# Splitting two output weights beside the first pass, and loading the parts at the change to the output pass

## The chip, the cores and the metric

The kernel runs on one core of a Trainium2 chip. The metric is the device time of one execution in microseconds (us). Engines are named as in the profile: PE (matrix products), DVE (vector), ACT (scalar), POOL (GpSimd) and SP, which here only starts transfers (DMAs). Each engine runs its instructions in the order of its own queue.

## The reference, cut to what matters

```python
def encoder_layer(x, ...):                      # 4096 + 2048 tokens, 1024 channels, float32
    h = rms_norm(x, pre_g)
    proj = jnp.einsum('bsd,de->bse', h, w_in)   # first pass: projections
    a_u, a_v, a_gate, b_in, b_gate, c_in, c_gate = jnp.split(proj, offsets, axis=-1)
    ya = mixer_a(a_u, a_v, ...) * jax.nn.silu(a_gate)
    yb = mixer_b(b_in, ...) * jax.nn.silu(b_gate)
    yc = mixer_c(c_in, c_w) * jax.nn.silu(c_gate)
    y = jnp.einsum('bse,ed->bsd', jnp.concatenate([ya, yb, yc], axis=-1), w_out)   # output pass
    return x + rms_norm(y, post_g)
```

## The kernel before

Big products are computed by a scheme with seven products in place of eight, called P1, P2, X1, X2, Y1, X3 and Y2. Each of the seven multiplies a sum of quadrants of the tokens by a sum of quadrants of the weights. To keep float32 accuracy, every factor is split into a high and a low part: `split` (L135 to L138) casts the source to the high part on ACT (L137) and subtracts it from the source on DVE (L138). `mm3` (L140) then makes three matmuls: high by high (L141), high by low (L142), low by high (L143).

The program has stages. The **first pass** takes 12 blocks of 512 tokens and ends near 485 us. The **b and a passes** follow until about 1358 us, in an order written by hand. The **output pass** takes 24 groups of 256 tokens, called q 0 to q 23, and ends the program. In the first and the output pass a scheduler of the compiler lays out each engine's queue from the order of the program and its own model of time.

In the first pass each block needs the statistics of its tokens. `row_squares(b+1)` is called in block b after P1. It loads four rows tiles (`xrow`, L362), each of which ACT squares in two halves with a sum (L365). The tiles take turns in a ring of **two** buffers (tag `xrow`). `statistics(b+1)` is called after X1: a sum and a scaling on DVE (L349, L351), a power on POOL (`rr`, L353), four diagonals on DVE (`diag`, L377), two matmuls that spread them (`prb`, L378), and a copy by ACT (`rbc`, L382). `normaliser` then multiplies the next block's operands (`xp`, L398) on DVE. The matmul outputs, `prb` among them, take turns in eight PSUM banks, given out in the order of the program.

Beside the blocks, `run_background` advances generators that prepare weights, one step after P2 and one after X3 of each block. `sum_weights("o", i, ...)` loads two rows tiles of the output weight (`wso0a` to `wso3b`, L741 and L742), makes four sums on POOL (L157 to L160), and stores the four results to `wall_o` in DRAM (L749).

At the change to the output pass, `load_out_weights` (L1513) loads each product's four summed tiles into places left by earlier weights (L1516), and `cut_out_weights` (L1519) splits each on the chip (L1522). The places have names such as `woY1h`, `woY2l`, `wol1`, `wo_more`. They name a place and not the product that uses it. The output group's operands (`yo_P`, `yo_Y`, `yo_X`) are made from `y` tiles loaded at L1533 and L1534, and split by ACT with DVE or POOL. Group q 0 also loads `pgb` (L1685) and scales it on DVE (L1686).

Of the kernel before, what the change touches and what calls it, by code (L numbers as in the profile page):

```python
# [10 lines left out]
F32 = mybir.dt.float32  # L11
F32R = mybir.dt.float32r
# [3 lines left out]
P = 128  # L16
D = 1024
NK = D // P
TB = 512
# [14 lines left out]
def hybrid_encoder(  # L34
# [33 lines left out]
    nc = tc.nc  # L68
# [6 lines left out]
    def pool(name, bufs):  # L75
        return phase.enter_context(tc.tile_pool(name=name, bufs=bufs, reuse_waits="tile"))
# [7 lines left out]
    w0g, wpa, e0, rpool, e1 = pool("w0g", 2), pool("wpa", 12), pool("e0", 1), pool("rpool", 1), pool("e0b", 1)  # L84
    hpool, xpool = pool("hpool", 6), pool("xpool", 8)
    dpool = ctx.enter_context(tc.tile_pool(name="dpool", bufs=1, space=DRAM))
# [22 lines left out]
    vn_d = dpool.tile([NTOK // P, P, 384], F32, name="vn_d")  # L109
    wb_d = dpool.tile([3, P, 1024], F32, name="wb_d")  # L110
    wall_d = {n: dpool.tile([7, P, c, TB], F32, name=f"wall_{n}") for n, c in (("b", 3), ("a", 3), ("o", 4))}
    z_d = [dpool.tile([s, 256], F32, name=f"z_d{i}") for i, s in enumerate(SEQS)]
    gc_d = [dpool.tile([256, s], F32, name=f"gc_d{i}") for i, s in enumerate(SEQS)]
    ya_d = [dpool.tile([384, s], F32, name=f"ya_d{i}") for i, s in enumerate(SEQS)]
# [21 lines left out]
    def split(src, hi, lo, pool_lo=False):  # L136
        last_cast[0] = nc.scalar.copy(hi, src)  # L137
        return (nc.gpsimd if pool_lo else nc.vector).tensor_sub(lo, src, hi.bitcast(F32))  # L138
# [16 lines left out]
    def weight_sums(b11, b12, b21, b22, eng):  # L155

        eng.tensor_sub(b11, b12, b11)  # L157
        eng.tensor_sub(b12, b22, b12)
        eng.tensor_sub(b22, b22, b11)
        eng.tensor_sub(b21, b21, b22)  # L160
# [247 lines left out]
    def row_tile(name):  # L408
        return rpool.tile([P, D], F32, tag="wrow", name=name, bufs=2)
# [325 lines left out]
    def place(name, m, i):  # L735
        return wall_d[name][OUT_ORDER.index(m)][:, i]

    def sum_weights(name, i, ra, rb):

        a, b_ = row_tile(f"ws{name}{i}a"), row_tile(f"ws{name}{i}b")  # L740
        nc.sync.dma_start(a, ra)  # L741
        nc.sync.dma_start(b_, rb)  # L742
        if name == "o":
            quads = a[:, W_H0], a[:, W_H1], b_[:, W_H0], b_[:, W_H1]
        else:
            quads = a[:, W_H0], b_[:, W_H0], a[:, W_H1], b_[:, W_H1]
        weight_sums(*quads, nc.gpsimd)
        for m, q in zip(("Y1", "X2", "X3", "X1"), quads):
            nc.sync.dma_start(place(name, m, i), q)  # L749
        yield  # L750

    background.extend(fold_pool_weights(h) for h in range(4))
    background.extend(sum_weights("b", t, wb_d[t], w1[2 + t]) for t in range(3))
    background.extend(sum_weights("a", t, w2[t], w2[3 + t]) for t in range(3))
    background.extend(sum_weights("o", k, w_o[k], w_o[k + 4]) for k in range(4))

    for b in range(NB):
# [755 lines left out]
    def load_out_weights(m):  # L1513
        hi, lo = ([next(place_of) for _ in range(4)] for _ in range(2))
        for k in range(4):
            nc.sync.dma_start(lo[k].bitcast(F32), wall_d["o"][OUT_ORDER.index(m)][:, k])  # L1516
        wo_raw[m] = hi, lo

    def cut_out_weights(m):  # L1519
        hi, lo = wo_raw.pop(m)  # L1520
        for k in range(4):
            split(lo[k].bitcast(F32), hi[k], lo[k])  # L1522
        wo[m] = list(zip(hi, lo))

    def load_y(q, yp=None):
# [52 lines left out]
    for b in range(NB // 2):  # L1578
# [42 lines left out]
        if b < NB // 2 - 1:  # L1621
            nxt = MixBlock(b + 1)
            ld[5].append(lambda n=nxt: n.load_v(0))
        else:
            for i, m in ((2, "P1"), (3, "X1"), (4, "P2"), (6, "X2")):
                ld[i].append(lambda m=m: load_out_weights(m))
                if m != "X2":
                    ct[i + 1].append(lambda m=m: cut_out_weights(m))
            ld[3].append(lambda: first_y.extend(load_y(0)))
            fb[5].append(next_y)  # L1630
            fb[6].append(next_y)
# [9 lines left out]
    prev.gate(0)  # L1641
    flush(stores)
    cut_out_weights("X2")
    assert at[0] > len(steps) + 1
    by_hand.close()
# [5 lines left out]
    for m in ("Y1", "X3", "Y2"):  # L1651
        load_out_weights(m)
        cut_out_weights(m)
        if m == "Y1":
            next_y()
# [241 lines left out]
```

## Time and profile before

| what | value |
|---|---|
| median of 3 runs | 1843.7 us |
| lowest and highest of them | 1839.59 and 1850.41 us |
| the profiled execution, its own time | 1844.26 us |
| its span, first to last instruction | 1842.5 us |
| mean granted TensorE clock (1 is 2.4 GHz) | 0.975 |
| PE busy | 1737.2 us, 94% |
| DVE busy | 1386.5 us, 75% |
| ACT busy | 915.9 us, 50% |
| POOL busy | 427.5 us, 23% |

An idle time in brackets stands at the instruction that ended it, with the engine and line that it had waited for. A busy share over the whole span mixes stages with different limits, so stretches are read one by one. PE is the fullest engine.

### The profile page before, as it was taken

How to read it: one execution, taken by the hardware profiler on the slowest of the kernel's cores; microseconds unless marked ns; L12 is line 12 of the kernel's file. 1: busy time of each engine (PE TensorE's matmuls, PEld its weight loads, DVE VectorE, ACT ScalarE, POOL GpSimd, SP SyncE). 2: the span in 40 equal slices, each digit the busy share in tenths (PEclk: the TensorE clock that was granted, in tenths of full speed). 3: DMA queues.
4: the chain of work that ended last, by engine and by line, in shares of the span. 5: the costliest groups of instructions: out<-in, count | busy, mean ns of one | idle time of the engine just before them, and what ended most of it. 6: DMA issues, size and time to landing. Idle time of an engine off the chain costs nothing. (4 is left out here: it accounts for less than half of the span.)

```text
span 1842.5 us, 27621 instructions
## 1 busy us (share of the span) xinstructions
PE 1737.2 (94%) x9784; PEld 1498.0 (81%) x9784; DVE 1386.5 (75%) x2320; ACT 915.9 (50%) x1766; POOL 427.5 (23%) x293
## 2 busy tenths in 40 slices
PE   5999999999998989799889999999989999999998
PEld 4999999999877777688677888778867888888886
DVE  8877777898588887667766677667776777777786
ACT  4766664335454554445545665646663433434332
POOL 5001121231000000000010100100115566665664
PEclk9999999999999999999899999999989999999999
DMA  6999997786868886879687577665934454454543
GB/s 248 324 335 342 350 358 273 278 309 250 281 227 272 279 306 246 275 273 306 231 291 266 198 241 255 221 219 168 310 124 161 161 170 162 160 170 162 171 149 114
DMA packets 221146, 443.83 MB, mean 241 GB/s; under 512 B 29776, under 2 KB 112336, under 8 KB 221008
## 3 DMA queue, kind: packets, MB, share of 16 engines
q1 hardware_dynamic: 221008, 442.07, 69.8%
q8 instruction: 77, 1.26, 0.3%
q14 instruction: 61, 0.50, 0.1%
HBM read 297.81 MB, written 150.47 MB: 243 GB/s over the span
## 5 line engine op out<-in xcount | busy, mean ns | idle before, releaser
L1421 POOL TENSOR_TENSOR lnst<-lnst,mhalf 128x16 f32<-128x16 f32 x12 | 38.2, 3180 | 525.5 <-DVE lnst L1420 289.2
L1729 POOL TENSOR_TENSOR cc<-cc,xr 128x1024 f32<-128x1024 f32 x46 | 110.3, 2398 | 53.5 <-DVE cc L1728 53.5
L398 DVE SCALAR_TENSOR_TENSOR xp<-xp,g_sb,rbc 128x256 f32<-128x256 f32 x192 | 97.5, 574 | 4.7 <-ACT rbc L382 3.2
L1432 ACT ACTIVATE vn<-vn,lnst 128x96 f32<-128x96 f32 x192 | 71.0, 456 | 43.7 <-DVE lnst L1427 42.5
L1670 ACT ACTIVATE junk<-cc 128x512 f32<-128x512 f32 x72 | 45.5, 632 | 86.0 <-DVE cc L1711 49.9
L137 ACT CAST yo_X<-y 128x512 fp32r<-128x512 f32 x60 | 34.9, 620 | 91.5 <-PE Xo L143 75.5
L138 DVE TENSOR_TENSOR yo_P<-y,yo_P 128x512 fp32r<-128x512 f32 x48 | 70.0, 1458 | 7.6 <-ACT yo_P L137 7.4
L1274 POOL MEMSET zb<- 128x16 f32 x6 | 0.5, 111 | 315.6 <-ACT zb L1272 254.3
L353 POOL TENSOR_TENSOR rr<-ssq,mhalf 128x4 f32<-128x4 f32 (+1 forms) x13 | 17.8, 1370 | 205.4 <-DVE ssq L351 118.5
L1728 DVE SCALAR_TENSOR_TENSOR cc<-cc,orr,pgb 128x512 f32<-128x512 f32 x69 | 53.8, 807 | 15.2 <-POOL orr L1678 15.2
L365 ACT ACTIVATE xrow<-xrow 128x512 f32<-128x512 f32 x88 | 54.9, 627 | 20.9 <-DMA xrow<-in_x_sample 20.0
L138 DVE TENSOR_TENSOR yo_X<-y,yo_X 128x512 fp32r<-128x512 f32 x48 | 58.9, 1226 | 0.2
L137 ACT CAST yo_P<-y 128x512 fp32r<-128x512 f32 x48 | 29.4, 615 | 47.1 <-PE Xo L143 26.1
L177 DVE TENSOR_TENSOR ys<-y,y 128x512 f32<-128x512 f32 x24 | 24.6, 1028 | 33.1 <-DMA y<-yc_d 32.9
L1417 DVE BATCH_NORM_STATS2 lnst<-vn 128x6 f32<-128x96 f32 x192 | 44.2, 230 | 6.3 <-ACT vn L1432 6.0
L1670 ACT ACTIVATE junk<-Po 128x512 f32<-128x512 f32 x24 | 14.4, 599 | 68.1 <-PE Po L143 68.1
L141 PE MATMUL pd<-mt,o 128*128 128x256 f32 (+1 forms) x80 | 27.0, 338 | 21.6 <-DMA mt<-const_m 18.6
L141 PE MATMUL Ab<-b_X1h,wbX1h 128*128 128x512 f32 x72 | 32.0, 444 | 15.7 <-ACT zb L1337 12.0
L1678 POOL TENSOR_TENSOR orr<-oms,mhalf 128x1 f32<-128x1 f32 x48 | 27.0, 563 | 84.1 <-DVE oms L1676 84.1
L1245 ACT COPY pa<-pb 32x512 f32<-32x512 f32 (+1 forms) x24 | 14.8, 619 | 56.6 <-DVE pb L1233 32.2
L1441 PE MATMUL pm<-ws,vn 128*32 128x128 f32 x1152 | 39.9, 290 | 2.8 <-ACT vn L1432 2.8
L1441 PEld LDWEIGHTS pm<-ws,vn 128*32 128x32 f32 x1152 | 34.6, 117 | 8.4 <-ACT vn L1432 5.5
(742 smaller groups left out, 6730.4 us busy)
## 6 DMA issues: line engine op xcount, KB each, us to landing
op_d<-xp SPq DMA_DIRECT2D x72, 512.0 KB, 5.1
mt<-const_m SPq DMA_DIRECT2D x56, 512.0 KB, 7.0
xp<-in_xt SPq DMA_DIRECT2D x48, 512.0 KB, 6.0
out<-cc SPq DMA_DIRECT2D x46, 512.0 KB, 2.9
xr<-in_x_sample SPq DMA_DIRECT2D x32, 512.0 KB, 4.3
xrow<-in_x_sample SPq DMA_DIRECT2D x28, 512.0 KB, 5.7
o<-o_d SPq DMA_DIRECT2D x40, 256.0 KB, 6.4
vn_d<-vg SPq DMA_DIRECT2D x48, 192.0 KB, 4.0
```

What stands on the lines that cost most here:

```text
L137: last_cast[0] = nc.scalar.copy(hi, src)
L138: return (nc.gpsimd if pool_lo else nc.vector).tensor_sub(lo, src, hi.bitcast(F32))
L141: nc.tensor.matmul(ps, lh, rh, start=first, stop=False, skip_group_check=True)
L365: nc.scalar.activation(half, half, AF.Square, accum_out=ss[:, 2 * c + h : 2 * c + h + 1])
L398: nc.vector.scalar_tensor_tensor(xs[q][:, sl], xs[q][:, sl], g8_sb[:, 4 * kh + k : 4 * kh + k + 1], rbc[a], ALU.mult, ALU.mult,)
L1417: nc.vector.bn_stats(st[:, j], self.v[h][c][:, 96 * hd : 96 * hd + 96])
L1421: nc.gpsimd.tensor_tensor(rv, va, mhalf, ALU.pow)
L1432: nc.scalar.activation(v_, v_, AF.Identity, bias=nb[:, j : j + 1], scale=rv[:, j : j + 1])
L1441: nc.tensor.matmul(pm[32 * hd : 32 * hd + 32, c * P : (c + 1) * P], self.v[h][c][:, 96 * hd + 32 * t : 96 * hd + 32 * t + 32], ws[:, hd], ...
L1670: nc.scalar.activation(junk, src, AF.Square, accum_out=ss[:, j : j + 1])
L1728: nc.vector.scalar_tensor_tensor(cc[c][:, hs], src, rr, pgb[:, hs], ALU.mult, ALU.mult)
L1729: nc.gpsimd.tensor_add(cc[c], cc[c], xr[c])
```

## The change

For the products Y1 and X3 of the output weight, `sum_weights` now also makes the high part beside the first pass. It takes a tile `whi` from the **same ring** as the `xrow` tiles, casts the sum into it on ACT, subtracts on DVE in place, and stores the high part to a new DRAM tensor `high_o`. `wall_o` then holds the low part for these two. `load_out_weights` loads the high part from there, and `cut_out_weights` leaves these two out. In all, 8 casts, 8 subtractions and 8 stores of 256 KB are added to the first pass, and at the change to the output pass 8 casts and 8 subtractions go and 8 loads of 256 KB come. Lines move by 2 (to about L748) and then by 6 to 9.

```diff
+    READY = ("Y1", "X3")
+    high_d = dpool.tile([len(READY), P, 4, TB], F32, name="high_o")
...
         for m, q in zip(("Y1", "X2", "X3", "X1"), quads):
+            if name == "o" and m in READY:
+                hi = e0.tile([P, D], F32, tag="xrow", name=f"whi{m}{i}", bufs=2)[:, 0:TB]
+                split(q, hi.bitcast(F32R), q.bitcast(F32R))
+                nc.sync.dma_start(high_d[READY.index(m)][:, i], hi)
             nc.sync.dma_start(place(name, m, i), q)
...
             nc.sync.dma_start(lo[k].bitcast(F32), wall_d["o"][OUT_ORDER.index(m)][:, k])
+            if m in READY:
+                nc.sync.dma_start(hi[k].bitcast(F32), high_d[READY.index(m)][:, k])
...
         for k in range(4):
-            split(lo[k].bitcast(F32), hi[k], lo[k])
+            if m not in READY:
+                split(lo[k].bitcast(F32), hi[k], lo[k])
```

The scheduler then lays out other queues. On PE before, in block 8 of the first pass, the two matmuls of the statistics of block 9 (`prb9`) stand between the gate columns (`Xg8`) of product X1 and the first matmul of X2.

```order
L143 MATMUL Xg8_4068<-p8_X1h_3958,wgX1l_181 128x256
L378 MATMUL prb9_4099<-diag9_0_4100,ident_146 128x256
L378 MATMUL prb9_4099<-diag9_1_4104,ident_146 128x256
L141 MATMUL Xc8_0_4042<-wtX2h_182,p8_X2h_4026 128x320
L142 MATMUL Xc8_0_4042<-wtX2l_183,p8_X2h_4026 128x320
```

On PE after, in the same block, they stand behind X3 (which now comes ahead of Y1), at the start of Y1 and within it.

```order
L145 MATMUL Xg8_4093<-p8_X3h_4176,wgX3l_194 128x256
L380 MATMUL prb9_4124<-diag9_0_4125,ident_147 128x256
L143 MATMUL Yc8_0_4180<-wtY1h_187,p8_Y1h_4114 128x320
...
L144 MATMUL Yc8_1_4193<-wtY1l_188,p8_Y1h_4114 128x320
L380 MATMUL prb9_4124<-diag9_1_4129,ident_147 128x256
L145 MATMUL Yc8_1_4193<-wtY1h_187,p8_Y1l_4115 128x320
```

So the statistics of block 9 stand some two products later, and X3 has moved ahead of Y1. The reason is seen on SP and ACT. On SP after, in the same block, the loads of the rows of block 9 (`xrow9`) are started between those of the weights (`wso2a`, `wso2b`), those of block 10's operands (`xp_10`) and the stores of the block's result (`z_d1`).

```order
L364 DMA xrow9_1_3984<-in_x_prompt 128x1024
L744 DMA wso2b_4048<-in_w_o 128x1024
L314 DMA xp_10_0_4373<-in_xt 128x1024
L314 DMA xp_10_1_4375<-in_xt 128x1024
L364 DMA xrow9_2_3988<-in_x_prompt 128x1024
...
L536 DMA z_d1_119<-ks1c8_1_3969 128x128
L364 DMA xrow9_3_3992<-in_x_prompt 128x1024
L755 DMA wall_o_116<-wso2a_4047 128x512
```

Before, all the `xrow` loads up to those of block 11 stood in the queue during blocks 3 to 5: the last, `xrow11_3`, stands just behind the stores of block 5. On ACT after, the squares of block 9 and the casts of the weights of steps 2 and 3 (`whiY12` is product Y1 of step 2) stand ahead of `rbc9` and of the first operand of block 9 (`p9_P1h`).

```order
L367 ACTIVATE xrow9_2_3988,ss8_9_3979<-xrow9_2_3988 128x512 x2
L139 CAST whiY12_4055<-wso2a_4047 128x512
L367 ACTIVATE xrow9_3_3992,ss8_9_3979<-xrow9_3_3992 128x512 x2
L139 CAST whiX32_4061<-wso2b_4048 128x512
L139 CAST whiY13_4307<-wso3a_4299 128x512
L535 ACTIVATE vg8_2_3926<-ku3c8_0_4170 128x192
L535 ACTIVATE vg8_3_3927<-ks1c8_1_3969 128x192
L384 COPY rbc9_4123<-prb9_4124 128x512
L139 CAST p9_P1h_4279<-xp_9_0_3915 128x1024
```

Nothing of the kind stood there before: ACT had `rbc9` right ahead of the cast `p8_Y2h`, with no squares and no weight casts near it.

On ACT before, at the change to the output pass (the operands `yo0` are those of q 0), the weight casts stand between the casts of the operands.

```order
L137 CAST yo0_Y1_13415<-ys3_0_13219 128x512
L137 CAST woY2l_13401<-wol1_13424 128x512 x2
L137 CAST yo0_Y1_13415<-y2_0_12942 128x512
L137 CAST woY1h_13291<-woY2h_13400 128x512
L137 CAST woY1l_13399<-woY2h_13400 128x512 x2
L137 CAST yo0_P2_13354<-y1_0_12941 128x512
...
L137 CAST woY1l_13399<-woY2l_13401 128x512
L137 CAST wol1_13424<-wol2_13425 128x512 x2
L137 CAST yo0_Y2_13487<-y2_0_12942 128x512
```

On ACT after, at the same place, eight of them are gone.

```order
L139 CAST yo0_Y1_13444<-ys3_0_13252 128x512
L139 CAST yo0_Y1_13444<-y2_0_12975 128x512
L139 CAST yo0_P2_13387<-y1_0_12974 128x512
...
L139 CAST woX3h_13322<-woX3l_13323 128x512 x2
L139 CAST woX3h_13322<-woY1h_13324 128x512
L139 CAST woX3l_13323<-woY1h_13324 128x512
L139 CAST yo0_Y2_13512<-y2_0_12975 128x512
```

The operands' casts move up by as many. DVE loses the eight subtractions that belong to them.

## Rows read from the trace of the kernel before

**Rows 1.** Page, busy time, share and instructions of PE and ACT.
```profile
PE 1737.2 (94%) x9784; PEld 1498.0 (81%) x9784; DVE 1386.5 (75%) x2320; ACT 915.9 (50%) x1766; POOL 427.5 (23%) x293
```

**Rows 2.** Windows: PE, PEld, DVE, ACT, POOL busy us; granted clock; DMA share; GB/s.
```profile
100.00:200.00 100.00, 100.00 (x735) 99.71 (x734) 73.61 (x138) 66.77 (x145) 7.29 (x4) 1.00 0.96 331
300.00:400.00 100.00, 95.03 (x674) 93.93 (x673) 83.36 (x119) 42.99 (x70) 26.36 (x19) 0.98 0.81 296
...
1370.00:1375.00 5.00, 3.82 (x9) 1.96 (x7) 5.00 (x10) 4.16 (x9) 1.77 (x1) 0.50 0.72 240
...
1400.00:1500.00 100.00, 99.89 (x437) 81.46 (x437) 77.48 (x95) 37.32 (x83) 63.99 (x43) 1.00 0.52 169
```

**Rows 3.** Waits of PE, 200 to 480 us: total, times, longest.
```profile
PE Pc L141 <- ACT ks1c L542: 6.5, 4, 2.3
PE Xc L141 <- ACT p_X1h L137: 2.7, 2, 1.5
```

**Rows 4.** Timeline of PE at a stop: start, us, instruction.
```profile
307.94 0.41 PE L141 MATMUL Pc<-wtP2h,p_P2h 128*128 128x320 f32 x1 [2.33 <-ACT ks1c L542]
...
309.20 0.47 PE L142 MATMUL Pc<-wtP2l,p_P2h 128*128 128x320 f32 x1
309.47 0.47 PE L143 MATMUL Pc<-wtP2h,p_P2l 128*128 128x320 f32 x1
```

**Rows 5.** Tile xrow, 100 to 480 us: duration in ns, minimum/median/maximum.
```profile
L365 ACT ACTIVATE xrow<-xrow x60: 612/625/647, 103.1 to 279.6; 128x512 f32<-128x512 f32 x60
L362 SPq DMA_DIRECT2D xrow<-in_x_prompt x16: 328/384/1412, 171.2 to 265.3; - x16
...
DMA to landing us min/median/max: 3.6/5.9/8.4
```

**Rows 6.** Groups of DVE, 100 to 480 us: busy us, mean ns.
```profile
L377 DVE TENSOR_SCALAR diag<-ident,rr 128x128 f32<-128x128 f32 x32 | 11.0, 393 | 2.2 <-PE prb L378 1.9
L559 DVE TENSOR_TENSOR ks1c<-Xc,ks1c 128x320 f32<-128x320 f32 x22 | 10.7, 485 | 1.4 <-PE Xc L143 1.3
...
L351 DVE TENSOR_SCALAR ssq<-ssq 128x4 f32<-128x4 f32 x8 | 1.3, 168 | 0.1
```

**Rows 7.** Line L353, 100 to 480 us, as rows 5.
```profile
L353 POOL TENSOR_TENSOR rr<-ssq,mhalf x8: 1006/1007/4274, 117.3 to 313.7; 128x4 f32<-128x4 f32 x8
```

**Rows 8.** Timeline of POOL, the last weight step.
```profile
422.32 1.78 POOL L157 TENSOR_TENSOR wso3a<-wso3a 128x512 f32<-128x512 f32 x1 [7.72 <-DMA wso3a<-in_w_o]
```

**Rows 9.** Timelines of DVE and ACT, normalising block 8's operands.
```profile
332.44 6.75 DVE L398 SCALAR_TENSOR_TENSOR xp<-xp,g_sb,rbc 128x256 f32<-128x256 f32 x9
...
338.91 1.05 ACT L137 CAST p_P2h<-xp 128x1024 fp32r<-128x1024 f32 x1 [7.70 <-DVE xp L398]
```

**Rows 10.** Timeline of PE at the change to the output pass.
```profile
1363.73 0.39 PE L143 MATMUL Xo<-woX1l,yo_P 128*128 128x512 f32 x1
1364.62 0.50 PE L141 MATMUL Yo<-woY1h,yo_Y 128*128 128x512 f32 x1 [0.50 <-ACT woY1h L137]
1368.39 0.80 PE L142 MATMUL Yo<-woY2h,yo_Y 128*128 128x512 f32 x1 [3.28 <-DVE woY2h L138]
...
1373.72 0.79 PE L141 MATMUL Po<-woP1h,yo_Y 128*128 128x512 f32 x1 [1.12 <-ACT yo_Y L137]
...
1387.81 0.80 PE L141 MATMUL Xo<-woY2l,yo_Y 128*128 128x512 f32 x1 [1.79 <-DVE u3o L1709]
...
1392.11 0.40 PE L143 MATMUL Xo<-woX1h,yo_X 128*128 128x512 f32 x1
```

**Rows 11.** Timeline of ACT at the same place.
```profile
1362.39 1.14 ACT L137 CAST woY2l<-wol 128x512 fp32r<-128x512 f32 x2
```

**Rows 12.** Timelines of POOL, SP and DVE at the same place.
```profile
1373.23 5.91 POOL L138 TENSOR_TENSOR yo_Y<-y,yo_Y 128x512 fp32r<-128x512 f32 x1 [41.02 <-DMA y<-ya_d]
...
1380.16 0.37 SPq L1685 DMA_DIRECT2D pgb<-in_post_g  x1
...
1386.46 0.69 DVE L1686 TENSOR_SCALAR pgb<-pgb 128x1024 f32<-128x1024 f32 x1 [7.89 <-issue]
```

## The prediction

> **What bounds the kernel now.** I read the busy shares first [rows 1]: PE is busy for 94% of the span, the next engine, DVE, for 75%. So the time moves where PE stops or runs slowly, and only there. The windows [rows 2] show where that is. From 100 to 200 us PE never stops, and its 735 matmuls give 0.136 us each, so one product of 36 matmuls takes 4.9 us. From 300 to 400 us it stops for 5 us. The output pass runs full. Between 1370 and 1375 us the granted clock is 0.50, the lower of the two levels (1.2 GHz). The waits of PE [rows 3] say what the first pass loses: 6.5 + 2.7 = 9.2 us in six waits from 200 to 480 us, all on ACT. The longest of them [rows 4] shows the second price of a stop: after 2.33 us without work, the matmuls of 320 columns start 0.27 us apart, and 12 or so of these, each 0.13 us above the mean of 0.136, make 1.6 us. At the change to the output pass [rows 10] the matmuls from 1363.73 to 1392.11 take 28.4 us; full speed is 100 / 437 = 0.229 us apart [rows 2], and the 62 of them would take 14.2. So the change costs about 14 us now. Its largest stop, 3.28 us, is for a weight's low part on DVE.
>
> **The change part by part: the casts and subtractions added.** Eight casts cost ACT about 0.57 us each (two took 1.14, [rows 11]), eight subtractions about as much on DVE. That is 4.6 us an engine, and ACT is idle for half of the span. I cost these at nothing by themselves. What counts is the ring they stand in.
>
> **The statistics of block 9.** The tiles `whi` of steps 0 and 1 stand in the two-buffer ring ahead of the rows tiles of block 9. Before, the squares of all blocks were over by 279.6 us [rows 5], some 60 us ahead of block 8's end. Now the four rows tiles of block 9 are loaded and squared within block 8, and the last load stands on SP behind two stores that need the end of Xc_1 X3 (the second half of the columns of product X3). From that end, PE still has the 12 gate matmuls of X3, 12 × 0.136 or about 1.5 us (they are the shorter ones), and then `prb9`. The path to `prb9` is: the last sum `ks1c`, 0.5 [rows 6]; two issues on SP at about 0.4 each (an issue took 0.37, [rows 12]), 0.8; the load, 5.9 in the median [rows 5]; two squares of 0.63, 1.3; two small operations of DVE at 0.17 [rows 6], 0.3; the power on POOL, 1.0 [rows 7]; two diagonals at 0.28 to 0.39, 0.7 [rows 6]. The sum is 10.5, less 1.5 for the cover: a stop of 9.0 us. With the shortest load of [rows 5], 3.6, it is 6.7; with the longest, 8.4, it is 11.5. The X3 matmuls were pulled ahead of Y1, so nothing is left behind them to fill it: Y1 needs a bank given out after `prb9`. Behind a stop of this length I count 2 us of slow matmuls (1.6 after the shorter stop of [rows 4]); bounds 0 and 3.
>
> The Trainium skill (DMA: Bandwidth & Descriptors, Anatomy of one DMA) fits 2.0 us plus the bytes over 436 GB/s to a DMA of GpSimd's path. For 512 KB that is an estimate of 3.2 us, and by it the stop would be 6.3 us and my forecast 1853 us. The median here, of SP's transfers with other transfers in flight, is 5.9, so the measurement decides and that sentence moves no term.
>
> **The operands of block 9.** The copy `rbc9` stands on ACT behind the cast of weight step 3, which waits for a load that starts only after step 2's stores. The last time, POOL waited 7.7 us for that load [rows 8]. With `prb9` at 10.5 after the end of Xc_1 X3, I put `rbc9` at about 17. PE has Y1 and Y2 until about 10.5 + 2 + 9.8 = 22.3. The first operand needs four multiplications and a cast and a subtraction, about 5 us: there in time. The second, P2, needs up to nine multiplications more, which took 6.75 us [rows 9], plus its cast and subtraction (2.2): ready at about 31.3, where P1 ends at 27.2. That is 4 us, and bounds of 0 and 6. In the trace of before ACT also waited for P2's operand, 7.70 us [rows 9], but there the chain began early enough. The X1 operand's cast then comes late too: 2 us, the size of the waits there now (2.7 in two, [rows 3]); bounds 0 and 3.
>
> **Other blocks.** Block 8 itself gets a cast and a subtraction ahead of its `ks1c` and `xp` work: +1 (0 to 2). Block 10's wait of P2, 1.6, goes (the four waits of [rows 3] are 1.0 to 2.3) and a wait of X1 of 1.0 comes: −0.6. Blocks 5 to 7 lose the squares and loads that stood there, and P2 is no longer cut in two by X1: the wait of 2.33 us at 307.94 [rows 4] goes, for −2 (0 to −4). The first pass sums to 9.0 + 2 + 4 + 2 + 1 − 0.6 − 2 = +15.4.
>
> **The change to the output pass.** ACT loses eight casts, 4.6 us, DVE eight subtractions, some 5 us. The stops of 0.50 and 3.28 us [rows 10] were for these. What is late next: the operand `yo_Y`, whose low part DVE makes after the casts (1.5), the low part of a remaining weight (0.5), the first matmul of P1 of q 1, whose `y` tile is loaded behind all weights, two more than before on that way (about 2; the cast of an operand from `y` held PE for 1.12 at 1373.72, [rows 10]), and half clock again for part of it. The last stop, 1.79 us on `u3o`, hangs on a chain of its own [rows 12]: POOL's `yo_Y` until 1379.1, then a `y` load, `pgb` at 1380.16, and its scaling at 1386.46. That chain starts from a cast on ACT which now comes some 2 to 3 us earlier, and it is bounded by that. Of the 14 us lost I take 4 back, with bounds of 2 and 6 (the whole of 0.50 + 3.28 and about 2 of slow clock).
>
> **Sum.** 15.4 − 4 = +11.4 on the profiled execution's 1844.26 us, which is 0.56 above the median of the runs. So 1855 us as a median. With every first-pass term at its low bound, the stop of 6.7 and nothing else but the −4.6 of the other blocks, and 6 back at the change, it is −3.9, or 1840; at the high bounds, 11.5 + 3 + 6 + 3 + 2 − 2 = +23.5, or 1867.
>
> On the slow matmuls, the rows show: PE without work for 2.33 us, then starts 0.27 us apart, about twice the mean of 0.136 [rows 2, 4]. The Trainium skill (TensorE: Matmul & The Clock Gate, The HAM clock gate) says that the clock of TensorE falls to 1.2 GHz when it idles. By this a stop costs more than its length, which speaks against the change, and each of the stops counted above (9 and 4 us) would pay it once; I have counted it for the first alone, and by both the sum would be 1857.
>
> **Rivals.** *The chain is hidden.* If the row loads land early, because the stores ahead of the last one go out at once, and the operands of block 9 are in time, only 6.7 stays, with 1 of slow clock, 1 in block 8, less 2.6: +6. Less 4 that is 1846, no change. For it: 3.6 us is a landing that was seen [rows 5], and PE's order gives P1 a good lead. Against: the DMA share is 0.81 there [rows 2]. *The chain comes back.* Blocks 10 and 11 have their rows just in time as well. If the stop comes again at block 10, at half its size, with late operands, +7: 1862. Against: their `prb` stand one product later than the last load. *Faster.* The six waits on ACT, 9.2 us, and their slow matmuls, some 4, come from a first pass in which squares and loads of later blocks share ACT and the queues with the blocks' own work (DMA share 0.96, [rows 2]). Moving them out could free all of it, and 6 come back at the change: 6.7 − 13 − 6, or −12, 1832; with half of it −6, 1838. It decides if the stop is below 6 us. Against: of the six waits only one lies in blocks that lose squares. *Nothing is saved at the change*, because the `y` and `pgb` loads take over at once: 1859. It is part of the range.
>
> **Chances.** The forecast 0.44, its own range 1849 to 1862; hidden 0.25; comes back 0.19; faster 0.12. A change within 0.5%, 9.2 us, can't be told from none. Of the forecast's 0.44 a quarter lies below 1853, so slower is 0.33 + 0.19 = 0.52; faster is three quarters of the last, 0.09; the rest, 0.39, is no change. The range takes in the forecast, the hidden chain and most of the one that comes back: 1842 to 1865.
>
> **What would show it.** Right: PE idle for 7 to 11 us before `prb9` in block 8 (waiting for DVE's `diag`), with a DMA `xrow` and ACT squares at the end of the chain; PE waiting for the P2 operand of block 9; the first pass longer by about 15 us; the 62 matmuls of the change in 22 to 26 us. Wrong: `prb9` without a wait of over 4 us, a first pass no longer than before, or a change to the output pass below 20 us.

## The result: 0.67% slower, at 1854.2 us

| | median | lowest to highest | ratio to before, 95% interval |
|---|---|---|---|
| before | 1841.49 us (8 runs) | 1838.18 to 1850.41 | |
| with the change | 1854.18 us (8 runs) | 1849.25 to 1862.38 | 1.0067 [1.0046, 1.0087] |

The profiled executions span 1842.5 and 1853.2 us. Cut into six stages on PE's timeline, the 10.7 us between them come from these:

| stage | before | after | difference |
|---|---|---|---|
| start to the first product (P1) of block 8 | 339.86 | 334.29 | −5.57 |
| block 8 | 36.67 | 56.44 | +19.77 |
| blocks 9 to 11 | 109.00 | 111.75 | +2.75 |
| b and a passes, to the first `Xo` | 875.70 | 872.14 | −3.56 |
| change to the output pass (first `Xo` to the last row of [rows 10]) | 30.88 | 27.63 | −3.25 |
| rest | 450.39 | 450.95 | +0.56 |

The first place to look is who PE waits for. This is the view of waits for PE from 200 to 480 us with the change, in total, times and longest, beside [rows 3].

```profile
PE prb L380 <- DVE diag L379: 8.5, 1, 8.5
PE Pc L143 <- ACT ks1c L544: 7.2, 4, 4.5
PE Yc L143 <- DVE ku3c L558: 3.1, 1, 3.1
PE Xc L143 <- DVE ku2c L547: 1.6, 1, 1.6
```

In [rows 3] there is no wait of `prb`. Now it heads the list. Block 8 alone, in the windows (the first row is of before; columns as in [rows 2]), shows both prices of a stop:

```profile
339.86:376.53 36.67, 35.64 (x258) 35.27 (x257) 32.47 (x47) 15.55 (x27) 10.56 (x8) 1.00 0.90 328
```

```profile
334.29:390.73 56.44, 38.82 (x246) 37.46 (x245) 34.75 (x53) 24.64 (x49) 18.49 (x13) 0.90 0.84 301
```

PE's time without work goes from 1.03 to 17.62 us, which is 16.6 of the 19.8 us. Its busy time for the same work goes from 35.64 to 38.82 while the granted clock falls from 1.00 to 0.90: that is the other 3.2.

The chain of the largest stop is read from the timelines of SP, ACT, DVE, POOL and PE in turn (start, us, instruction; in brackets the idle time before it and what ended it).

```profile
365.60 0.30 PE L145 MATMUL Xc<-wtX3h,p_X3l 128*128 128x320 f32 x1
```

```profile
365.07 1.71 SPq L536 DMA_DIRECT2D z_d<-ks1c  x2
366.87 0.38 SPq L364 DMA_DIRECT2D xrow<-in_x_prompt  x1
```

```profile
365.94 0.61 ACT L367 ACTIVATE xrow<-xrow 128x512 f32<-128x512 f32 x1
...
372.40 0.63 ACT L367 ACTIVATE xrow<-xrow 128x512 f32<-128x512 f32 x1 [2.01 <-DMA xrow<-in_x_prompt]
```

```profile
374.21 1.01 POOL L355 TENSOR_TENSOR rr<-ssq,mhalf 128x4 f32<-128x4 f32 x1 [5.64 <-DVE ssq L353]
```

```profile
375.25 0.87 DVE L379 TENSOR_SCALAR diag<-ident,rr 128x128 f32<-128x128 f32 x4
```

```profile
375.79 0.79 PE L380 MATMUL prb<-diag,ident 128*128 128x256 f32 x1 [8.51 <-DVE diag L379]
388.20 0.41 PE L143 MATMUL Yc<-wtY2h,p_Y2h 128*128 128x320 f32 x1 [3.11 <-DVE ku3c L558]
```

Xc_1 X3 ends at about 365.9. The last row load starts at 366.87 behind the two stores of the block's result, its tile is squared from 372.40, POOL's power starts at 374.21, and `prb` at 375.79, 9.9 us after the end of X3. The stores are not the only thing that held this load. The last row tile takes the ring place of the tile two before it, whose second square ran from 365.94 to 366.55 (with the read of its sum, 366.65): 0.2 us ahead of the load.

The second line of PE's timeline is the stop of Y2. It waits for DVE's `ku3c`, and DVE's queue has the reason: four multiplications of `xp` stand ahead of it, and they wait for `rbc`, which ACT could copy only behind a weight cast.

```profile
384.00 3.74 DVE L400 SCALAR_TENSOR_TENSOR xp<-xp,g_sb,rbc 128x256 f32<-128x256 f32 x4 [3.75 <-ACT rbc L384]
387.67 0.48 DVE L558 TENSOR_TENSOR ku3c<-Yc,ku3c 128x320 f32<-128x320 f32 x1
```

```profile
382.36 0.62 ACT L139 CAST whiY<-wso3a 128x512 fp32r<-128x512 f32 x1 [7.92 <-POOL wso3a L159]
...
383.41 0.57 ACT L384 COPY rbc<-prb 128x512 f32<-128x512 f32 x1
```

The four multiplications were slow too. They ran beside POOL's sums of weight step 3 and took 3.74 us; the same four took 1.66 in block 8 of before, with POOL idle. The difference is 2.1 of the 3.11 us.

```profile
361.82 1.66 DVE L398 SCALAR_TENSOR_TENSOR xp<-xp,g_sb,rbc 128x256 f32<-128x256 f32 x4
```

At the start of the same block, two stops of P2 add up to 5.99 us (1.03 before). DVE's two operations there took 2.14 and 2.30 us, where 1.22 is their usual time, while two sums of weight step 1 ran on POOL, each at 2.1 us in place of 1.3. Then ACT's cast of that step stood right ahead of the `ks1c` that PE waited for.

```profile
339.20 2.14 DVE L140 TENSOR_TENSOR p_P2l<-xp,p_P2h 128x1024 fp32r<-128x1024 f32 x1
341.27 2.30 DVE L179 TENSOR_TENSOR s<-xp,xp 128x1024 f32<-128x1024 f32 x1
```

```profile
340.34 2.15 POOL L161 TENSOR_TENSOR wso1b<-wso1b,wso1a 128x512 f32<-128x512 f32 x1
342.57 2.13 POOL L162 TENSOR_TENSOR wso1b<-wso1b 128x512 f32<-128x512 f32 x1
```

```profile
346.64 0.60 ACT L139 CAST whiX<-wso1b 128x512 fp32r<-128x512 f32 x1
347.15 0.42 ACT L544 COPY ks1c<-Pc 128x320 f32<-128x320 f32 x1
```

These stops took back what PE had gained ahead of block 8. The second half of P2 starts at the same time in both kernels (first line before, second after):

```profile
347.71 0.42 PE L141 MATMUL Pc<-wtP2h,p_P2h 128*128 128x320 f32 x1 [1.03 <-ACT ks1c L542]
```

```profile
347.62 0.41 PE L143 MATMUL Pc<-wtP2h,p_P2h 128*128 128x320 f32 x1 [4.48 <-ACT ks1c L544]
```

PE came to block 8 5.6 us earlier, but DVE began P2's low part only 2.6 us earlier (339.20 for 341.82). Of these 2.6 us, DVE's two slow operations took 2.0 and the cast on ACT 0.5.

At the change to the output pass, the rows of PE's timeline that answer to [rows 10] are these.

```profile
1377.55 0.40 PE L145 MATMUL Xo<-woX1l,yo_P 128*128 128x512 f32 x1
...
1379.22 0.49 PE L144 MATMUL Yo<-woY2h,yo_Y 128*128 128x512 f32 x1 [1.05 <-DMA woY2h<-wall_o]
1380.15 0.50 PE L145 MATMUL Yo<-woY1h,yo_Y 128*128 128x512 f32 x1 [0.43 <-DVE yo_Y L140]
...
1387.04 0.80 PE L143 MATMUL Po<-woP1h,yo_Y 128*128 128x512 f32 x1 [3.95 <-ACT yo_Y L139]
...
1402.25 0.39 PE L145 MATMUL Xo<-woX1h,yo_X 128*128 128x512 f32 x1
```

The 62 matmuls take 24.7 us (28.4 before). The windows of this stretch, before and after (columns as in [rows 2]), show where the 3.7 us come from:

```profile
1363.73:1392.11 28.38, 20.85 (x65) 14.67 (x64) 17.94 (x30) 11.77 (x24) 9.72 (x4) 0.76 0.52 176
```

```profile
1377.55:1402.25 24.70, 18.42 (x64) 13.37 (x63) 13.73 (x23) 8.44 (x17) 8.22 (x4) 0.86 0.66 235
```

PE's time without work fell by only 1.3 us (7.53 to 6.28); the other 2.4 are matmuls that ran less at the low clock (0.76 to 0.86). The stop of 3.28 us on a weight's low part is gone, and one of 3.95 has come. Its cause is a load, as ACT's timeline says:

```profile
1386.37 0.62 ACT L139 CAST yo_Y<-y 128x512 fp32r<-128x512 f32 x1 [3.87 <-DMA y<-yb_d]
```

### The profile page after: what moved, and what is told of

It reads as the page before. It is cut to its first block, busy times and chain, and to the rows that moved or that the text cites. A ratio compares the mean times of both kernels' runs of the same rounds, so it can differ in the third digit from the quotient of the medians.

```text
span 1853.2 us, 27649 instructions
## 1 busy us (share of the span) xinstructions
PE 1735.4 (94%) x9784; PEld 1494.8 (81%) x9784; DVE 1377.6 (74%) x2320; ACT 917.1 (49%) x1766; POOL 438.7 (24%) x293
## 5 line engine op out<-in xcount | busy, mean ns | idle before, releaser
L400 DVE SCALAR_TENSOR_TENSOR xp<-xp,g_sb,rbc 128x256 f32<-128x256 f32 x192 | 81.9, 492 | 7.6 <-ACT rbc L384 6.3
L193 POOL TENSOR_TENSOR y<-y,y 128x512 f32<-128x512 f32 x23 | 33.7, 1465 | 33.2 <-DVE yo_X L140 30.8
```

The source lines that it names most:

```text
L400: nc.vector.scalar_tensor_tensor(xs[q][:, sl], xs[q][:, sl], g8_sb[:, 4 * kh + k : 4 * kh + k + 1], rbc[a], ALU.mult, ALU.mult,)
```

## The experiments

Theory RING: the high parts take places in the two-buffer ring of the rows tiles, so the rows of blocks 9 to 11 come late. Rival WORK: the eight casts, subtractions and stores cost by themselves. For the saving at the change, the rival is TAKEOVER: another wait takes what is gained. All ratios are to the kernel before, with 95% intervals.

**Weight steps put off.** Six turns that do nothing are put ahead of the steps, so that in the program they come after the rows of every block, with the ring as it is:

```diff
+    background.append(pause(6))
     background.extend(sum_weights("o", k, w_o[k], w_o[k + 4]) for k in range(4))
```

> The whole change, but the four steps that sum the output weight are put off by six turns in the program, so that all tiles of high parts stand in the ring of two behind the rows tiles of every block. The same casts, subtractions and stores are in the first pass. Theory RING (what costs is that the rows of blocks 9 to 11 wait for ring places held by the weights' high parts): the rows run ahead again, no wait of prb for diag above 1 us, the first b-pass product starts at 485 to 489 us (before 485.5, with the change 502.5), and the time is 2 to 4 us below before. Rival WORK (the eight casts, subtractions and stores cost by themselves): the first pass stays 8 to 17 us longer and the time stays near that of the change, +8 to +13.

Measured: 1834.18 us, 0.9951 [0.9932, 0.9969]. No wait of `prb`; the b pass starts at 481.45, and the change takes 27.19 us in place of 30.88. PE's waits from 200 to 480 us:

```profile
PE Pc L143 <- ACT ks1c L544: 4.9, 3, 2.3
PE Xc L143 <- ACT p_X1h L139: 1.8, 2, 1.5
```

The same casts, subtractions and stores are in the first pass, so WORK falls. The saving is larger than either theory gave: the first pass is also 4.1 us shorter than before, half of it in block 10 (35.18 for 37.22), where the P2 stop of 1.55 us is gone with another order on PE. That part was not expected and is not tested further.

**High parts in the weight's own tile.** The stores of X2 and X1 go first, and their halves of the tile then take the high parts:

```diff
-                hi = e0.tile([P, D], F32, tag="xrow", name=f"whi{m}{i}", bufs=2)[:, 0:TB]
+                hi = parts["X2" if m == "Y1" else "X1"]
```

> The whole change, but each high part is written into a half of the weight's own tile that an earlier store has freed, not into the ring of the rows tiles. RING: first pass as before within 3 us (b pass from 485 to 489 us), the change to the output pass 3 us shorter, in all 1 to 4 us below before. WORK: first pass 8 to 17 us longer, in all +5 to +13. A third possibility: the steps get slower by two landings (about 8 us each), since the high part waits for a store to land, and then something else waits for them.

Measured: 1835.12 us, 0.9964 [0.9949, 0.998], a little more below before than the 1 to 4 us expected; b pass from 483.98, change 27.70 us, no wait of `prb`. RING holds by a second way, with the steps where the change had put them in the program. The scheduler put the weight steps late again as well: POOL's first sum of step 1 ran at 394.6 us (335.9 with the change, 384.8 before). So that they had come earlier was the ring's doing too.

**The ring alone.** The kernel before, with eight casts into the ring and nothing else:

```diff
+            if name == "o" and m in ("Y1", "X3"):
+                hi = e0.tile([P, D], F32, tag="xrow", name=f"whi{m}{i}", bufs=2)[:, 0:TB]
+                nc.scalar.copy(hi.bitcast(F32R), q)
             nc.sync.dma_start(place(name, m, i), q)
```

> The kernel before with only eight casts of weights into tiles of the rows' ring: no subtractions, no stores of high parts, the change to the output pass as before. RING: the rows of blocks 9 to 11 come late again; here the last row load of block 9 stands ahead of the two stores of block 8's result, so the stop before prb9 is smaller than 8.5 us, 3 to 8; the first pass 6 to 14 us longer than before, the change to the output pass as long as before (28 us for 62 matmuls), in all +5 to +14. WORK: within 3 us of before.

Measured: 1848.33 us, 1.0034 [1.0012, 1.0055]; b pass from 492.95, 7.4 us later than before. Here the last row load of block 9 stood ahead of the two stores (357.04 against 365.65 us on SP), and the stop was smaller, as expected:

```profile
370.15 0.80 PE L378 MATMUL prb<-diag,ident 128*128 128x256 f32 x1 [3.45 <-DVE diag L377]
```

So the places in the ring make the loss, 7.4 of the 17.0 us by themselves. The rest comes only with the subtractions and stores, which cost nothing in the two runs above: here the first two row loads of block 9 started one behind the other from 348.75, with the change at 349.83 and 355.92. That a stored high part holds its place until its store has landed would explain this, but no run tests it. That the stores of the block's result set the size of the stop is not shown by this run: here the last row tile was not late by its load, but squared behind other work in ACT's queue (at 366.77, behind `vg` and a weight cast). The stop of P2 in block 8 was there too (4.99 us), with nothing subtracted or stored: ACT's cast waited for a sum of an earlier weight step, and `ks1c` stood behind the cast.

```profile
343.67 0.62 ACT L751 CAST whiX<-wso1b 128x512 fp32r<-128x512 f32 x1 [5.53 <-POOL wso1b L160]
344.19 0.42 ACT L542 COPY ks1c<-Pc 128x320 f32<-128x320 f32 x1
```

**The second half alone.** The eight tiles are loaded twice and not split:

```diff
+            if m in ("Y1", "X3"):
+                nc.sync.dma_start(hi[k].bitcast(F32), wall_d["o"][OUT_ORDER.index(m)][:, k])
...
-            split(lo[k].bitcast(F32), hi[k], lo[k])
+            if m not in ("Y1", "X3"):
+                split(lo[k].bitcast(F32), hi[k], lo[k])
```

> The kernel before with only the second half of the change: at the change to the output pass, the eight tiles are loaded twice and not split (both parts are the raw sum, so the split of Y1 and X3 is left out and the first pass does none of it). Theory: the 62 matmuls take 25 us in place of 28.2, in all 2 to 4 us below before; first pass unchanged. Rival TAKEOVER (the y and pgb loads take over at once): 28 us again, in all within 1 us. Rival FULL: 14 to 20 us, 8 or more below before.

Measured: 1838.65 us, 0.9974 [0.9958, 0.999]; change 27.77 us (30.88 before). The saving is real and about 3 us. PE's waits from 1355 to 1405 us show what is next in line:

```profile
PE Po L141 <- ACT yo_Y L137: 4.1, 1, 4.1
PE Yo L143 <- DVE yo_Y L138: 1.2, 1, 1.2
```

**The parts made on POOL.** Same ring, but POOL casts and subtracts:

```diff
-                split(q, hi.bitcast(F32R), q.bitcast(F32R))
+                nc.gpsimd.tensor_copy(hi.bitcast(F32R), q)
+                nc.gpsimd.tensor_sub(q.bitcast(F32R), q, hi)
```

> The whole change with the same ring, but the high and low parts are made on POOL, so that ACT and DVE have none of them in their queues beside the first pass. Theory, term by term: the stop before prb9 stays (the last row load of block 9 still stands behind the stores of block 8's result), 7 to 9 us; the stop before Y2 of block 8 (3.1 us) goes, as the copy of the statistics no longer stands behind a weight cast on ACT; the stop of P2 in block 8 (6.0 us in two) shrinks to below 3, if the weight cast on ACT caused it, or stays, if POOL's sums beside DVE caused it. First pass 8 to 13 us longer than before, in all +2 to +8. Rival (the casts and subtractions on ACT and DVE hold the rows, the ring does not): the stop before prb9 goes too.

Measured: 1856.39 us, 1.008 [1.006, 1.0101]. The Y2 stop is gone, and P2's stops fell from 5.99 us in two to one of 3.05, with ACT now waiting for a store of `ks1c` there. That the casts on ACT caused the Y2 stop does not follow: `rbc` was copied no earlier (383.64 for 383.41), and what changed is that the four multiplications took 1.67 us in place of 3.74, with no sum on POOL beside them, and that PE came later. And block 8 took 56.42 us, as with the change (56.44): the stop before `prb` grew by as much.

```profile
377.31 1.22 PE L380 MATMUL prb<-diag,ident 128*128 128x256 f32 x2 [13.56 <-DVE diag L379]
```

PE came 3.5 us earlier to a chain that ended 1.5 us later. The last row's squares began as with the change (372.24 for 372.40), but DVE's two small operations behind them took 0.50 and 1.19 us beside POOL's last sum and first subtraction, in place of 0.16 and 0.17; POOL was free for the power just as they ended.

```profile
373.60 0.50 DVE L351 TENSOR_TENSOR ssq<-ss 128x4 f32<-128x4 f32 x1 [9.39 <-ACT xrow L367]
374.13 1.19 DVE L353 TENSOR_SCALAR ssq<-ssq 128x4 f32<-128x4 f32 x1
```

```profile
374.04 1.26 POOL L754 TENSOR_TENSOR wso2a<-wso2a,whiY 128x512 fp32r<-128x512 f32 x1
375.40 1.01 POOL L355 TENSOR_TENSOR rr<-ssq,mhalf 128x4 f32<-128x4 f32 x1
```

This run also says what held the last row load. The two stores were out at 363.3, yet the load started at 368.19, when the squares of the tile two before it, in the same ring place, were over. Here the place held it, and not the stores.

```profile
361.69 1.59 SPq L536 DMA_DIRECT2D z_d<-ks1c  x2
368.19 0.33 SPq L364 DMA_DIRECT2D xrow<-in_x_prompt  x1
```

```profile
367.46 0.61 ACT L367 ACTIVATE xrow<-xrow 128x512 f32<-128x512 f32 x1
```

The stops of block 8 are therefore not independent terms: what PE gains ahead of the chain, it waits for there. The expected 7 to 9 us, and the total of +2 to +8, were wrong for these two reasons.

**Rows paced.** The steps put off, and a ring tile in each block that is written from a sum of the block before:

```diff
+                    pace = e0.tile([P, D], F32, tag="xrow", name=f"pace{b}", bufs=2)
+                    nc.vector.tensor_copy(pace[:, 0:1], before_u2[:, 0:1])
                 nsq = row_squares(b + 1)
```

> The kernel with the weight steps put off, and a tile of the rows' ring in each block that is written from a sum of the block before, so that the rows of the next block cannot be loaded more than a block ahead (a write of 1 column on DVE per block is added). Theory EASED (the rows and squares that ran far ahead cost blocks 5 to 7 about 5 us; with the change these blocks were that much shorter): blocks 5 to 7 take 35 to 36 us in place of 37, 36 and 39, and the time is 3 to 6 us below the kernel with the steps put off (1834), 1828 to 1831. Rival (it was the place of the weight steps, or the rows one block ahead cost as much in each later block): 1832 to 1840.

Measured: 1853.18 us, 1.0057 [1.0039, 1.0075]. EASED falls. Blocks 5 to 7 took 110.9 us together (112.0 with the steps merely put off), and block 8 took 43.1, since PE's order now had X1 ahead of P2 with squares in front of its cast:

```profile
PE Xc L143 <- ACT p_X1h L139: 8.3, 4, 5.5
```

The loss is not a price that each block pays for its rows: block 9, with 12 squares in it, took 35.6 us, and block 10, with none, 35.3. Of the 10.2 us by which the b pass starts later than with the steps merely put off, 6.4 are in block 8 and 3.5 in the last block. With the change, blocks 5 to 7 had no squares, and blocks 8 and 9 had those of three blocks.

**The y load earlier.** The steps put off, and one more buffer for `y`, so that group 1's load waits for no place:

```diff
-            (yp if i == 2 and yp else mtpool).tile([P, 4, HB], F32, tag="mt", name=f"y{i}_{q}") for i in (1, 2)
+            (yp if (i == 2 or q == 1) and yp else mtpool).tile([P, 4, HB], F32, tag="mt", name=f"y{i}_{q}") for i in (1, 2)
...
-    wpool["more"], wpool["y"] = pool("wmore", 1), pool("ypool", 2)
+    wpool["more"], wpool["y"] = pool("wmore", 1), pool("ypool", 3)
```

> The kernel with the weight steps put off, and one more buffer for the operands' sources at the change to the output pass, so that the load of group 1 stands ahead of the last weights' loads and waits for no place. Theory TAKEOVER (what took over at the change is this load: PE waits 3.8 to 4.2 us for the cast behind it): that wait falls below 1 us, the stretch from the first matmul of Xo to the last of group 0's half takes 24 to 25 us in place of 27.2, and the time is 2 to 3 us lower, 1831 to 1833. Rival: another wait (the remaining weights, the pgb chain) takes the 3.8 us, and the time stays at 1834.

Measured: 1831.54 us, 0.9941 [0.9924, 0.9959]. The change takes 25.14 us (27.19 without the buffer). PE's waits from 1345 to 1400 us:

```profile
PE Po L145 <- DVE yo_Y L140: 2.9, 1, 2.9
PE Yo L144 <- DMA woY2h<-wall_o: 1.8, 1, 1.8
PE Po L143 <- ACT s1o L1715: 1.1, 1, 1.1
```

The wait for the cast behind the load is gone, so TAKEOVER by that load is shown; 2 of its 3.8 us were saved, and DVE's low part, a weight load and `s1o` took the rest. Its median is the lowest of all here, 10 us below before; its interval overlaps that of the steps put off alone.

**Both of the last two.**

> Both of the last two. If each holds, the savings add, since one is in the first pass and one at the change to the output pass: 1826 to 1829. If neither, 1834 or more.

Measured: 1849.89 us, 1.0041 [1.0025, 1.0057]. The change took 25.84 us against 27.95 for the paced kernel without the buffer, so that saving adds; the paced first pass loses as before, and the 1826 to 1829 us expected did not come.

## Why the prediction was right, step by step

The total (1855 forecast, 1854.2 measured) is nearer than its terms. The largest term held with its mechanism, and so did the saving at the change. Of the other terms of the first pass, two came out near by another path, and two missed their bounds and cancelled.

- **The stop before `prb9`:** forecast 9.0 us with a path of 10.5, measured 8.51 with 9.9. Load, squares, power and diagonals were each near the rows they were taken from: the load from its start to the first square took 5.5 (5.9 forecast). The prediction let the load hang on the stores alone; its ring place came free only 0.2 us before, and with the parts made on POOL the place was what held it. (In the kernel before, the squares were over some 60 us ahead of block 8's start, not of its end; no term hangs on that.)
- **Slow matmuls:** forecast 2 behind this stop, measured 3.2 for all of block 8's stops; the share of this one was not measured apart. Behind the 8.51 us without work, from 376 to 379 us, the granted clock was 0.50, the lower level (1.2 GHz; row below). That agrees with the rule of the Trainium skill (TensorE: Matmul & The Clock Gate, The HAM clock gate) that the clock drops to 1.2 GHz when TensorE idles.

```profile
376.00:379.00 3.00, 3.00 (x11) 2.82 (x12) 0.13 (x1) 0.00 (x0) 0.00 (x0) 0.50 0.93 249
```

- **`rbc9` late behind a weight cast:** forecast at about 17 us after X3's end, measured 17.5 (383.41). But who waits was wrong. I had P2's operand of block 9 (4 us); it was never waited for. Y2 of block 8 waited 3.11, because DVE's `ku3c` stood behind the multiplications for block 9, and 2.1 us of that was their slowness beside POOL. I had counted Y2 as PE's cover. The size was near for another reason than mine.
- **X1 late, +2:** block 9 lost 2.2 us in stops, but only 0.27 + 0.29 of them on X1. The 1.63 on X2 hang on DVE's `ku2c`, behind an operand whose cast stood on ACT behind squares of block 10's rows (406.58). Again the size was near and the path another. Block 10 gained 0.4 (0.6 forecast), with a wait of 1.24 on Y1 and none on X1.
- **Block 8 itself, +1:** the worst term, and outside its bounds of 0 to 2. P2 stopped for 5.99 us, 5.0 more than before. I had priced the added cast and subtraction, and not that PE would come early to operands that were not, nor that the weight steps, which also came earlier, ran their POOL sums beside DVE's work on P2.
- **Blocks to 7, −2:** measured −5.57, outside the bounds of 0 to −4. Block 7, whose stop of 2.33 us the term was for, gave 2.3. Blocks 5 and 6 gave 1.7 and 1.2: their waits of X1 (1.53 and 1.14) went too. I had read that one wait lay in blocks that lose squares; squares ran until 279.6, in both. So two misses of about 4 us in the first pass cancelled: 15.4 forecast, 16.95 measured. They are in the main one miss seen twice, since block 8's P2 waited for what the blocks ahead had gained; that the two came out so nearly equal (347.71 and 347.62) is luck, as far as the traces show.
- **The change to the output pass, −4:** measured −3.25, and 24.7 us for the 62 matmuls (22 to 26 forecast). The load that took over is the one named, at 3.95 in place of 2; the slow clock took 2.4 us less (2 at the high bound).
- **Nothing forecast in the b and a passes:** −3.56 there. No product of these was changed (the first loads of the high parts start there, at 1355). The same stretch took 871 to 886 us in the profiles of the experiments (879.6 with an unchanged first pass), and the largest single difference from before is a wait for a `mt` load (8.29 and 5.35 us). I take it for the spread of loads; that it is chance is not shown.
- **The rivals:** a second stop at block 10 didn't come (its `prb` didn't wait). "Hidden" and "nothing saved" are refuted by the two waits above. The rival that the first pass would be eased had a true core, the 5.6 us ahead of block 8, but PE had waited for all of it by the second half of block 8's P2.

## What to carry to other kernels

A tile that borrows a place in a small ring also takes a place in that ring's order: ask which tiles come after it, and how far they ran ahead until now. Look where the scheduler then puts the dependent matmul, and sum the path to it, stores that share its queue and the tile that holds its place included; several stops that hang on one late chain do not add, since time saved ahead of it is waited for at it. Here the borrowed place was free of cost once the borrowing steps stood behind all rows.

## What was not expected of the hardware

The same operation on DVE (elementwise, on two tiles of 128x1024) took 1.22 us alone and, in block 8 with the change, 2.14 to 2.30 us while POOL ran sums of 128x512, which took 2.1 in place of 1.3 us. There the two engines together did some 1.2 times the work of one (an estimate: 1.22 / 2.2 + 1.3 / 2.1). It was not always both: in the kernel before, one such operation took 2.31 us (at 359.59) beside a POOL sum at 1.35, and another 1.22 (at 384.50) beside a POOL sum at 2.11. What decides who loses was not tested.
